# A rotary embedding on half of each head: three 8.4 MB slots with 64 KB rows on one DMA queue, instead of six 4.2 MB buffers with 32 KB rows

## The chip, the cores and the metric

The kernel runs on one core of one Trainium2 chip. The metric is the device time of one execution in microseconds (us). The profile's span is about 1.8 us shorter than that time (160.6 beside 162.34 us for the profiled run of the kernel before); spans are compared with spans only. All timed runs quoted are in the fast state with a granted clock of 1.0, except the two kernels named `gap_...`, which were run once and whose state is therefore unknown.

Executions of one kernel on one chip scatter by about 0.3 us, and now and then by more (one execution of the kernel before took 163.91 us). Each experiment was timed beside the kernel before, and that kernel's own median moved from 161.96 to 162.51 us between the sets of runs; times of different sets are compared by their ratio to the kernel before.

## The reference, cut to what matters

```python
# x: (16, 512, 16, 64) float32; cos, sin: (512, 32) float32
half_dim = 32
x1, x2 = x[..., :32], x[..., 32:]                # x2 is passed through
first  = x1[..., :16] * cos[..., :16] - x1[..., 16:] * sin[..., :16]
second = x1[..., :16] * sin[..., :16] + x1[..., 16:] * cos[..., :16]
return concatenate([first, second, x2], axis=-1)
```

x has 33.55 MB. Every byte comes in from HBM and goes out again, whether it is rotated or not: 67.1 MB for the DMA.

## The kernel before

A tile is 128 partitions by 32 KB (4.19 MB); there are eight tiles and six buffers. Six loads are queued at once. Each tile is rotated in place by four VectorE instructions, with PSUM as the scratch, and stored. Loads 6 and 7 wait for the store that frees their buffer. The constants come over GpSimd's queue.

```python
    K = 8
    NB = 6
    # ... views of x and out as (tile, partition, 8192 elements)
    nc.gpsimd.dma_start(out=stage[:, 0]..., in_=cosf)
    nc.gpsimd.dma_start(out=stage[:, 1]..., in_=sinf)
    # ... table = the constants spread to 128 partitions, four copies
    for t in range(NB):
        load(t)                                   # nc.sync.dma_start, 32 KB per partition
    for t in range(T):
        x1 = x_t[:, :, :, 0:HF]
        nc.vector.tensor_mul(out=b_t[:], in0=x1, in1=s)
        nc.vector.tensor_mul(out=x1, in0=x1, in1=c)
        nc.vector.tensor_sub(out=x1[..., 0:Q], in0=x1[..., 0:Q], in1=b_t[..., Q:HF])
        nc.vector.tensor_add(out=x1[..., Q:HF], in0=x1[..., Q:HF], in1=b_t[..., 0:Q])
        nc.sync.dma_start(out=of[t], in_=x_t...)
        if t >= 1 and t - 1 + NB < T:
            load(t - 1 + NB)
```

## Time and profile before

| | us |
|---|---|
| median of the first three runs | 162.21 (162.18 to 162.48) |
| span of the profiled run | 160.6 |
| VectorE busy | 107.9 (67%) |
| DMA queue q1, share of 16 engines' span | 97.8% |

From the page of the kernel before: busy time, the DMA row in 40 slices of 4 us (tenths of busy share, and GB/s), and the DMA queues (packets, MB, share).

```profile
span 160.6 us, 118 instructions
DVE 107.9 (67%) x36; POOL 1.4 (1%) x6
DVE  0025999999999999999999999982999000000000
DMA  7999999999999999999999999999999999999994
GB/s 245 424 408 392 424 490 392 392 514 400 392 465 449 392 392 482 433 392 449 465 392 433 433 441 408 449 441 416 441 441 408 441 449 416 441 441 424 416 449 180
DMA packets 2368, 67.24 MB, mean 419 GB/s; under 512 B 288, under 2 KB 288, under 8 KB 320
q1 hardware_dynamic: 2304, 67.11, 97.8%
```

The DMA row is full but for the first and last slice: the kernel is DMA-bound throughout. VectorE ends 36 us before the span does, so its idle time costs nothing. 2304 packets on q1 are 2048 of 32 KB and 256 that count semaphores.

The instruction groups of the kernel before, costliest first: line, engine, operation, shapes | busy us, mean ns | idle before and what ended it.

```profile
L73 DVE TENSOR_TENSOR b_t<-x_t,table 128x4096 f32<-128x4096 f32 x8 | 35.5, 4432 | 5.7 <-DMA x_t<-in_x_dram 5.5
L49 DVE COPY table<-stage 64x256 f32<-64x256 f32 x4 | 1.1, 287 | 10.6 <-DMA stage<-in_cos_dram 8.4
```

**The four sections that this text uses.** The trace keeps start, duration and size of every DMA packet. I cut each span at four points that can be read from them: the *head* (span start to the first packet of x), the *first phase* (the 25.2 MB of x, 6 x 4.19 MB, until the last of their packets has ended), the *rest* (the other 41.9 MB) and the *tail* (last packet's end to the end of the span). This is my arithmetic on the packet records, not a view of the profile. In the trace of before: head 1.75, first phase 60.36, rest 97.23, tail 1.23 us; together 160.57. In steady stretches a further 4.19 MB of loads takes 9.71 us and of stores 9.68 us.

### The profile page before, as it was taken

To read this page: it belongs to the slowest core of one execution; us is meant where nothing else is said; L and a number is where in the kernel's file an instruction comes from. 1 tells how busy PE (TensorE), PEld (TensorE's weight loads), DVE (VectorE), ACT (ScalarE), POOL (GpSimd) and SP (SyncE) were. 2 spreads that over 40 slices of the span, in tenths; PEclk is the share of its full clock that TensorE was granted. 3 is DMA by queue.
4 is the path that set the end of the run, shared out by engine and by line. 5 is a ranking of instruction groups with operands and counts; after the bars stand their busy time and mean duration, and the time that the engine had idled before them with its cause. 6 is when DMAs were issued, how large, how long until landed. Compare 5 with 4: busy or idle time off the path is not lost.

```text
span 160.6 us, 118 instructions
## 1 busy us (share of the span) xinstructions
DVE 107.9 (67%) x36; POOL 1.4 (1%) x6
## 2 busy tenths in 40 slices
DVE  0025999999999999999999999982999000000000
POOL 3000000000000000000000000000000000000000
DMA  7999999999999999999999999999999999999994
GB/s 245 424 408 392 424 490 392 392 514 400 392 465 449 392 392 482 433 392 449 465 392 433 433 441 408 449 441 416 441 441 408 441 449 416 441 441 424 416 449 180
DMA packets 2368, 67.24 MB, mean 419 GB/s; under 512 B 288, under 2 KB 288, under 8 KB 320
## 3 DMA queue, kind: packets, MB, share of 16 engines
q1 hardware_dynamic: 2304, 67.11, 97.8%
q0 software_dynamic: 64, 0.13, 0.2%
HBM read 33.69 MB, written 33.55 MB: 419 GB/s over the span
## 4 chain that ended last, share of the span: by engine, by line
DMA 52%; DVE 21%; issue 3%; DVEq 1%
DMA x_t<-in_x_dram 26%; DMA out_dram<-x_t 26%; DVE b_t L73 8%; DVE x_t L74 8%; DVE x_t L78 3%; DVE x_t L75 2%; DVEq L109 1%; DVEq L73 0%
## 5 line engine op out<-in xcount | busy, mean ns | idle before, releaser
L73 DVE TENSOR_TENSOR b_t<-x_t,table 128x4096 f32<-128x4096 f32 x8 | 35.5, 4432 | 5.7 <-DMA x_t<-in_x_dram 5.5
L74 DVE TENSOR_TENSOR x_t<-x_t,table 128x4096 f32<-128x4096 f32 x8 | 35.4, 4424 | 0.3
L75 DVE TENSOR_TENSOR x_t<-x_t,b_t 128x2048 f32<-128x2048 f32 x8 | 18.3, 2286 | 0.3
L78 DVE TENSOR_TENSOR x_t<-x_t,b_t 128x2048 f32<-128x2048 f32 x8 | 18.2, 2279 | 0.0
L49 DVE COPY table<-stage 64x256 f32<-64x256 f32 x4 | 1.1, 287 | 10.6 <-DMA stage<-in_cos_dram 8.4
L42 POOL DMA_DIRECT2D stage<-in_cos_dram x1 | 0.6, 648 | 0.8 <-PEq L109 0.8
L43 POOL DMA_DIRECT2D stage<-in_sin_dram x1 | 0.5, 518 | 0.0
L98 POOL MEMSET const-bfloat16-1.0<- 128x1 bf16 x1 | 0.1, 102 | 0.0
L98 POOL MEMSET const-float32-0.0<- 128x1 f32 x1 | 0.1, 98 | 0.2 <-issue 0.2
L98 POOL MEMSET const-float32-1.0<- 128x1 f32 x1 | 0.1, 99 | 0.0
L98 POOL MEMSET const-uint8-127<- 128x1 uint8 x1 | 0.1, 99 | 0.0
## 6 DMA issues: line engine op xcount, KB each, us to landing
x_t<-in_x_dram SPq DMA_DIRECT2D x8, 4096.0 KB, 30.2
out_dram<-x_t SPq DMA_DIRECT2D x8, 4096.0 KB, 41.9
stage<-in_cos_dram POOLq DMA_DIRECT2D x1, 64.0 KB, 7.2
stage<-in_sin_dram POOLq DMA_DIRECT2D x1, 64.0 KB, 9.3
```

Of the source, the lines that this page charges most:

```text
L42: nc.gpsimd.dma_start(out=stage[:, 0].rearrange("p k j -> p (k j)"), in_=cosf)
L43: nc.gpsimd.dma_start(out=stage[:, 1].rearrange("p k j -> p (k j)"), in_=sinf)
L49: nc.vector.tensor_copy(out=table[r * PB : (r + 1) * PB, t], in_=stage[:, t, :, 0:Q].unsqueeze(2).to_broadcast((PB, K, 2, Q)),)
L73: nc.vector.tensor_mul(out=b_t[:], in0=x1, in1=s)
L74: nc.vector.tensor_mul(out=x1, in0=x1, in1=c)
L75: nc.vector.tensor_sub(out=x1[:, :, :, 0:Q], in0=x1[:, :, :, 0:Q], in1=b_t[:, :, :, Q:HF])
L78: nc.vector.tensor_add(out=x1[:, :, :, Q:HF], in0=x1[:, :, :, Q:HF], in1=b_t[:, :, :, 0:Q])
L98: nc = _bacc.Bacc("TRN2", target_bir_lowering=False, num_devices=1)
L109: with _tile.TileContext(nc) as tc:
```

## The change

Its intent: the same bytes with half as many, twice as long rows, everything on one queue. Three slots of 8.39 MB; the constants come behind load 0 in the same queue; the first tile is stored in halves so that the last tile can be loaded into its place in halves; then three whole stores.

```diff
-    K = 8
+    K = 16
-    NB = 6
+    NS = 3
+    KC = K // 2
-    nc.gpsimd.dma_start(out=stage[:, 0]..., in_=cosf)
-    nc.gpsimd.dma_start(out=stage[:, 1]..., in_=sinf)
+    ring = const_pool.tile([P, NS, K, H, D], fp32)
+    load(0)
+    nc.sync.dma_start(out=stage[:, 0]..., in_=cosf)
+    nc.sync.dma_start(out=stage[:, 1]..., in_=sinf)
+    load(1)
+    load(2)
     # (the table's copies: four of 32x1024 instead of four of 64x256)
-    for t in range(NB):
-        load(t)
-    for t in range(T):
-        # ... rotate tile t
-        nc.sync.dma_start(out=of[t], in_=x_t...)
-        if t >= 1 and t - 1 + NB < T:
-            load(t - 1 + NB)
+    rotate(0, 0)
+    store(0, 0, KC)
+    rotate(0, KC)
+    store(0, KC, K)
+    load(3, 0, KC)
+    load(3, KC, K)
+    for t in range(1, T):
+        rotate(t, 0)
+        rotate(t, KC)
+        store(t)
```

(The moved body of the rotation is the same.)

More of the change, by code (lines that the diff above doesn't have):

```diff
@@ L29 @@
     REP = P // PB
-    NB = 6
+    R = H * D
+    NS = 3
+    KC = K // 2
     xf = x.rearrange("b s h d -> (b s h d)").rearrange("(t p f) -> t p f", t=T, p=P)
@@ L37, with rows @@
     const_pool = ctx.enter_context(tc.tile_pool(name="const", bufs=1))
-    x_pool = ctx.enter_context(tc.tile_pool(name="xp", bufs=NB))
     b_pool = ctx.enter_context(tc.tile_pool(name="bp", bufs=1, space=bass.MemoryType.PSUM))
+    ring = const_pool.tile([P, NS, K, H, D], fp32)
     stage = const_pool.tile([PB, 2, K, HF], fp32)
-    nc.gpsimd.dma_start(out=stage[:, 0].rearrange("p k j -> p (k j)"), in_=cosf)
-    nc.gpsimd.dma_start(out=stage[:, 1].rearrange("p k j -> p (k j)"), in_=sinf)
     table = const_pool.tile([P, 2, K, 2, Q], fp32)
-    for r in range(REP):
-        for t in range(2):
-            nc.vector.tensor_copy(
-                out=table[r * PB : (r + 1) * PB, t],
-                in_=stage[:, t, :, 0:Q].unsqueeze(2).to_broadcast((PB, K, 2, Q)),
-            )
+    def rows(t, lo, hi):
+        return ring[:, t % NS, lo:hi].rearrange("p k h d -> p (k h d)")
@@ new lines, in load, with store @@
+    def load(t, lo=0, hi=K):
+        nc.sync.dma_start(out=rows(t, lo, hi), in_=xf[t, :, lo * R : hi * R])
+    def store(t, lo=0, hi=K):
+        nc.sync.dma_start(out=of[t, :, lo * R : hi * R], in_=rows(t, lo, hi))
+    load(0)
+    nc.sync.dma_start(out=stage[:, 0].rearrange("p k j -> p (k j)"), in_=cosf)
+    nc.sync.dma_start(out=stage[:, 1].rearrange("p k j -> p (k j)"), in_=sinf)
+    load(1)
+    load(2)
+    for r in range(REP):
+        nc.vector.tensor_copy(
+            out=table[r * PB : (r + 1) * PB].rearrange("p t k c j -> p (t k) c j"),
+            in_=stage.rearrange("p t k j -> p (t k) j")[:, :, 0:Q]
+            .unsqueeze(2)
+            .to_broadcast((PB, 2 * K, 2, Q)),
+        )
@@ L53 @@
     C = table[:, 0].rearrange("p k c j -> p k (c j)")
     Sn = table[:, 1].rearrange("p k c j -> p k (c j)")
-    KC = 8
-    tiles = []
-    def load(t):
-        x_t = x_pool.tile([P, K, H, D], fp32, name="x_t")
-        nc.sync.dma_start(out=x_t.rearrange("p k h d -> p (k h d)"), in_=xf[t])
-        tiles.append(x_t)
-    for t in range(NB):
-        load(t)
-    for t in range(T):
-        x_t = tiles[t]
-        for k0 in range(0, K, KC):
-            x1 = x_t[:, k0 : k0 + KC, :, 0:HF]
-            c = C[:, k0 : k0 + KC].unsqueeze(2).to_broadcast((P, KC, H, HF))
-            s = Sn[:, k0 : k0 + KC].unsqueeze(2).to_broadcast((P, KC, H, HF))
-            b_t = b_pool.tile([P, KC, H, HF], fp32)
-            nc.vector.tensor_mul(out=b_t[:], in0=x1, in1=s)
-            nc.vector.tensor_mul(out=x1, in0=x1, in1=c)
-            nc.vector.tensor_sub(
-                out=x1[:, :, :, 0:Q], in0=x1[:, :, :, 0:Q], in1=b_t[:, :, :, Q:HF]
-            )
-            nc.vector.tensor_add(
-                out=x1[:, :, :, Q:HF], in0=x1[:, :, :, Q:HF], in1=b_t[:, :, :, 0:Q]
-            )
-        nc.sync.dma_start(out=of[t], in_=x_t.rearrange("p k h d -> p (k h d)"))
-        if t >= 1 and t - 1 + NB < T:
-            load(t - 1 + NB)
@@ new lines, in rotate @@
+    def rotate(t, k0):
+        x1 = ring[:, t % NS, k0 : k0 + KC, :, 0:HF]
+        c = C[:, k0 : k0 + KC].unsqueeze(2).to_broadcast((P, KC, H, HF))
+        s = Sn[:, k0 : k0 + KC].unsqueeze(2).to_broadcast((P, KC, H, HF))
+        b_t = b_pool.tile([P, KC, H, HF], fp32)
+        nc.vector.tensor_mul(out=b_t[:], in0=x1, in1=s)
+        nc.vector.tensor_mul(out=x1, in0=x1, in1=c)
+        nc.vector.tensor_sub(
+            out=x1[:, :, :, 0:Q], in0=x1[:, :, :, 0:Q], in1=b_t[:, :, :, Q:HF]
+        )
+        nc.vector.tensor_add(
+            out=x1[:, :, :, Q:HF], in0=x1[:, :, :, Q:HF], in1=b_t[:, :, :, 0:Q]
+        )
```

## The prediction

> **What bounds the kernel now.** The DMA engines. The DMA part of the profile's page shows queue q1 busy for 97.8% of 16 engines' span and 419 GB/s over 160.6 us; VectorE is busy 107.9 us (67%) and finishes at 124.7 us (timeline), 36 us before the end. In the trace's packet records a 32 KB packet takes 1213 ns (27.0 GB/s an engine); steady completions of successive 4.19 MB transfers are 9.68 us apart for stores and 9.71 us for loads, 433 and 432 GB/s. The Trainium skill, "DMA: Bandwidth & Descriptors", section "Where 436 GB/s comes from", gives 435.2 GB/s as the fabric's ceiling; this trace agrees to 0.7%. So 67.1 MB need 154.2 us at that ceiling and took 155.3 us plus about 2.3 us of extras: first transfer 1.7 us late (ramp, first packets 2.0 us instead of 1.2; constants in between) and about 0.8 us at the three places where a load is followed by a store. Head (1.75 us to the first packet) and tail (1.2 us after the last) are the rest.
>
> **What the change does.** The same bytes go through. It halves the number of big packets (2048 of 32 KB to mostly 64 KB), cuts x transfers from 16 to 10, moves the constants from the GpSimd queue behind the first 8.4 MB load, and enlarges the tiles from 4.19 to 8.39 MB in three slots. VectorE's rotations keep their shapes: 13.44 us per half, 107.6 us in all. The table copies grow: four of 32x1024 where four of 64x256 took 287 ns; estimate from that, at equal time per element, 1.1 us each, 4.5 us.
>
> **What lies on the critical path.** Only DMA continuity and packet efficiency. My schedule (estimates from these durations, us): load 0 and constants landed at 23.5; rotation from 28 to 136 without a pause; queue: load 1 and 2 to 62; store 0a and 0b 62 to 81; load 3a and 3b 81 to 101; store 1 to 120; store 2 to 140; store 3 to 159. Store 0a is ready at 41, 0b at 55; load 3a waits for 0a to land (about 72) while 0b still runs, load 3b waits for 0b while 3a runs; store 3 is ready at 136, 3 to 4 us before the engines reach it. So no bubble, and later VectorE work costs nothing.
>
> Gain: a packet costs 5 (stores) to 9 (loads) ns over its bytes at 435.2 GB/s; the skill's same page, section "Why small descriptors are slow", names a fixed cost of some cycles per packet. Up to 64 fewer packets an engine: 0.3 to 0.6 us, estimate 0.45. One load-to-store turn fewer and less interference of the constants: 0.2 us. Total -0.65 us of 162.2: 161.5 us, -0.4%.
>
> So 161.5 us, range 160.9 to 162.4; faster by over 2%: 0.02, within 2%: 0.94, slower by over 2%: 0.04.
>
> **What would show it right or wrong.** Right: about 1100 to 1400 packets; 64 KB packets near 2418 ns; DMA share 9 in every slice but the ends; VectorE idle about 27 us at the start, then busy to about 136 us; SP waits only, with DMA never idle. A DMA gap near 72 to 85 us would show load 3 waiting too long; one near 140 us, the last store coming too late.
>
> **What would make it wrong.** 64 KB runs cut into 32 KB packets (gain shrinks to 0.2 us); 64 KB packets or their larger row pitch running slower than 27 GB/s an engine; the constants landing late, or table copies far slower than estimated, so that the 3 to 4 us of slack before store 3 are gone; a longer ramp or slower turns.

## The result, and the profile after

| | before, us | after, us | ratio, 95% interval |
|---|---|---|---|
| first measurement, 6 runs each | 162.29 | 162.09 | 0.9987 [0.9969, 1.0004] |
| again, 11 and 6 runs | 162.22 | 161.92 | 0.9967 [0.9933, 1.0001] |

A ratio is the mean time of one kernel's fast runs over that of the other's in the same rounds, so it isn't quite the ratio of the medians. The gain is some 0.2 to 0.3 us, where 0.65 us was forecast; each interval just reaches 1.

The page of the changed kernel, the same lines as above:

```profile
span 160.2 us, 103 instructions
DVE 109.5 (68%) x36; POOL 0.2 (0%) x4
DVE  0000009999999999999999999999999995000000
DMA  8969989699699797999999999996996996996990
GB/s 262 524 262 524 524 295 524 262 524 507 278 524 475 311 524 327 458 393 434 483 393 401 483 425 393 524 524 262 524 507 278 524 507 278 524 491 295 524 491 33
DMA packets 1536, 67.24 MB, mean 420 GB/s; under 512 B 192, under 2 KB 192, under 8 KB 256
q1 hardware_dynamic: 1536, 67.24, 98.0%
```

The sixes and the swing from 262 to 524 GB/s are not gaps. A packet is counted in the slice in which it starts; sixteen engines start their 64 KB packets (2.42 us) almost together, so a 4 us slice holds sometimes one set, sometimes two. The packet records show all engines at work without a gap. Packets fell from 2368 to 1536, and the mean rate is 420 GB/s after 419. The work is the same, done at almost the same rate.

```profile
L79 DVE TENSOR_TENSOR b_t<-ring,table 128x4096 f32<-128x4096 f32 x8 | 35.5, 4432 | 0.3
L65 DVE COPY table<-stage 32x1024 f32<-32x1024 f32 x4 | 2.7, 683 | 23.9 <-DMA stage<-in_sin_dram 23.9
```

Those are the groups of the changed kernel. VectorE waits 23.9 us for the constants and then works without a pause until 134.2 us (timeline). The waits of the queue's own engine show that the stores were in the queue in time:

```profile
SPq L55 <- DVE ring L84: 80.8, 4, 26.5
SPq L52 <- DMA out_dram<-ring: 27.9, 2, 18.1
```

(Engine, line, what it waited for: us in total, times, longest.) SP waits long, but the DMA always has queued work meanwhile. The last store is issued at 134.2 us, and its packets start from 138.9 us on.

Here are the four sections for both kernels, two traces each, in us:

| | before | before, again | after | after, again | after - before, first pair / second pair |
|---|---|---|---|---|---|
| head | 1.75 | 1.74 | 1.74 | 1.75 | 0.00 / +0.01 |
| first phase (25.2 MB) | 60.36 | 60.43 | 60.12 | 60.15 | -0.24 / -0.28 |
| rest (41.9 MB) | 97.23 | 97.49 | 96.92 | 96.87 | -0.30 / -0.62 |
| tail | 1.23 | 1.23 | 1.41 | 1.40 | +0.18 / +0.18 |
| span | 160.57 | 160.89 | 160.19 | 160.17 | -0.37 / -0.72 |

(The profiled run of the second "before" was 162.66 us, above its kernel's median of 162.49, so the second pair overstates the gain.) Steady loads now take 9.675 us per 4.19 MB (9.71 before), and whole stores 9.66 us (9.68). That is the per-packet gain that was predicted: 6 x 0.039 + 6 x 0.022 = 0.37 us. But the 0.23 us that the loads contribute lie wholly in the first phase. That phase did become 0.24 to 0.28 us shorter, but the run with the old rows in the new order (runs_32k, below) is shorter by as much.

### The profile page after: what moved, and what is told of

It reads as the page before. It is cut to its first block, busy times and chain, and to the rows that moved or that the text cites. A ratio compares the mean times of both kernels' runs of the same rounds, so it can differ in the third digit from the quotient of the medians.

```text
span 160.2 us, 103 instructions
## 1 busy us (share of the span) xinstructions
DVE 109.5 (68%) x36; POOL 0.2 (0%) x4
## 2 busy tenths in 40 slices
DMA packets 1536, 67.24 MB, mean 420 GB/s; under 512 B 192, under 2 KB 192, under 8 KB 256
## 3 DMA queue, kind: packets, MB, share of 16 engines
q1 hardware_dynamic: 1536, 67.24, 98.0%
## 4 chain that ended last, share of the span: by engine, by line
DVE 61%; DMA 14%; issue 6%; DVEq 1%; SPq 0%
DVE b_t L79 22%; DVE ring L80 22%; DMA stage<-in_sin_dram 14%; DVE ring L84 10%; DVE ring L81 6%; DVE table L65 1%; DVEq L123 1%; SPq L58 0%; SPq L52 0%; DVEq L65 0%
## 5 line engine op out<-in xcount | busy, mean ns | idle before, releaser
L79 DVE TENSOR_TENSOR b_t<-ring,table 128x4096 f32<-128x4096 f32 x8 | 35.5, 4432 | 0.3
L80 DVE TENSOR_TENSOR ring<-ring,table 128x4096 f32<-128x4096 f32 x8 | 35.4, 4424 | 0.3
L65 DVE COPY table<-stage 32x1024 f32<-32x1024 f32 x4 | 2.7, 683 | 23.9 <-DMA stage<-in_sin_dram 23.9
L81 DVE TENSOR_TENSOR ring<-ring,b_t 128x2048 f32<-128x2048 f32 x8 | 18.3, 2286 | 0.3
L84 DVE TENSOR_TENSOR ring<-ring,b_t 128x2048 f32<-128x2048 f32 x8 | 18.2, 2279 | 0.0
```

The source lines that it names most:

```text
L65: nc.vector.tensor_copy(out=table[r * PB : (r + 1) * PB].rearrange("p t k c j -> p (t k) c j"), in_=stage.rearrange("p t k j -> p (t k) j" ...
L81: nc.vector.tensor_sub(out=x1[:, :, :, 0:Q], in0=x1[:, :, :, 0:Q], in1=b_t[:, :, :, Q:HF])
L84: nc.vector.tensor_add(out=x1[:, :, :, Q:HF], in0=x1[:, :, :, Q:HF], in1=b_t[:, :, :, 0:Q])
```

## The experiments

Two words for what follows: a *turn* is the place in the queue where a load is followed by a store, and a *stall* is what the last load packets of a run take beyond their steady time, averaged over the 16 engines.

### Repeats, and the constants moved

> The kernel before, unchanged, for the scatter. From its first trace: data 157.59 us from the first to the last 32 KB packet, head 1.75, tail 1.23 us; in the data, beyond a steady 9.71 us (load) and 9.68 us (store) per 4.19 MB: start 1.68 us, the three load-to-store turns 0.40, 0.28 and 0.11 us. If these terms are properties of the kernel they return within 0.1 us; if they are chance[...] they move by some tenths. Ratio 1.000 within 0.002.

> The changed kernel, unchanged, five rounds. Theory 1 (bookkeeping of the first trace): packets -0.37, turns -0.6, start with constants +0.41, tail +0.18, sum -0.37 us, ratio 0.9977. Rival: the first trace's turns were luck, sum near -0.1 us, ratio 0.9993. The trace is expected to show steady 9.675 us per 4.19 MB for loads and 9.66 for stores, and about 0.8 us of extra where the constants pass.

Measured: before again 162.49 us (ratio 1.0003 to itself), after again 161.92 us. The medians of identical kernels differ by up to 0.27 us (162.49 against 162.22), which is the scatter to keep in mind. In the traces the terms of before did move. Its start term (time to 4.19 MB beyond the steady 9.71) was 1.68 and then 2.14 us, and its first turn took 0.40 and then 0.01 us extra. Their sum, 2.08 and 2.15 us, hardly moved. That was the first hint. The two forecasts for the repeat of the changed kernel, ratios of 0.9977 and 0.9993, both lie in the measured interval (0.9933 to 1.0001), so the times don't decide between them. Its trace repeats: every section returned within 0.06 us, and the steady rates as well.

```diff
# const_gpsimd: the changed kernel with
-    nc.sync.dma_start(out=stage[:, 0]..., in_=cosf)      # between load(0) and load(1)
+    nc.gpsimd.dma_start(out=stage[:, 0]..., in_=cosf)    # sin likewise
```

> The changed kernel with the constants back on the GpSimd queue, wanted early. Theory 1: a burst of 2 KB packets between two loads in one queue costs 0.34 us of its own and then about 0.5 us of slow first packets of load 1; on the other queue they overlap the start: start term 2.08 falls to about 1.65, time -0.4 us against the changed kernel. Rival: constants cost the same wherever they pass (0.3 to 0.8 us): the start term stays within 0.15 us of 2.08 and the time is equal.

Measured: 162.33 us (ratio 0.9996), nothing gained over before. What the start cost stayed at 2.05 us (1.63 + 0.42), as the rival said; theory 1 fell. The rest grew to 97.25 us.

```diff
# const_first: the changed kernel with
-    load(0)
     nc.sync.dma_start(out=stage[:, 0]..., in_=cosf)
     nc.sync.dma_start(out=stage[:, 1]..., in_=sinf)
+    load(0)
```

> The changed kernel with the constants first in the same queue, before load 0. Theory 1: the slow first packets come once after every burst of small packets or idle stretch, so here they are paid once only: start term about 1.3 us (0.34 for the constants, 0.9 for the slow first packets), time -0.7 us against the changed kernel less what the two extra issues put before load 0 (0.9 us of issue, partly hidden). Rival: the issue time of the two constants delays load 0 by its full 0.9 us, so nothing or +0.2 us.

> The kernel with the constants first, once more, for a second trace. If the 1.32 us at the turn after load 2 belongs to this order it returns (above 0.9 us); if it was chance it falls among the 0.0 to 0.4 us of the other kernels and the time is about 1 us shorter than 163.5.

Measured: 163.52 us (ratio 1.0077) and 163.13 us (1.0061): slower, with both intervals above 1, though by less than 2%. The head grew from 1.74 to 2.69 us, because load 0 is issued behind the two small transfers. The start term did fall by 0.9 to 1.0 us, to 1.08 and 1.23 us. But then load 2 ended 1.32 and 1.09 us later than its steady rate gives, because its last packets were slow. The saving before the turn was taken back at the turn.

### Run length and tail, each alone

```diff
# runs_32k: every load and store of the changed kernel in two halves (32 KB rows)
     def load(t, lo=0, hi=K):
+        if hi - lo > KC:
+            load(t, lo, lo + KC)
+            load(t, lo + KC, hi)
+            return
```

> The changed kernel with every 64 KB transfer cut into its two 32 KB halves, order, queue, table and slots as in the changed kernel: the run length alone undone. Theory 1 (run length is worth its per-packet cost): steady 9.71 us per 4.19 MB for loads and 9.68 for stores again, data +0.37 us over the changed kernel's 157.03, and the tail back from 1.41 to 1.23 us, so about +0.2 us in time, 162.2. Theory 2 (fewer slow turns come with the 64 KB runs): the turns grow from 0.15 back to 0.6 to 0.8 us as well, about +0.7 us. Rival (turns follow from the order of transfers): turns stay near 0.15 us.

Measured: 162.03 us, ratio 0.9979 [0.9961, 0.9998] to before. So the changed order with the old row length does as well as the changed kernel. Steady rates went back to 9.71 and 9.68 us, the rest to 97.07 (+0.2), the tail to 1.19 (-0.2). The first phase stayed at 60.155 us although it had 0.23 us more of packet cost in it. So the 64 KB rows do what was predicted per packet, but set against this run they gain only 0.14 to 0.20 us, all of it in the rest, and the tail takes back 0.21. In the time they bring nothing measurable.

```diff
# tail_halves: the changed kernel, the last store in halves
-        store(t)
+        store(t) if t < T - 1 else (store(t, 0, KC), store(t, KC, K))
```

> The changed kernel with only the last store cut into two 32 KB-run halves. Theory: the longer tail (1.41 against 1.23 us from the last packet's end to the end of the span) comes with the 64 KB packets at the end; it returns to 1.23, data +0.02, time -0.15 us, 161.8. Rival: the tail comes from the 8.4 MB size or from chance and stays at 1.4.

Measured: 162.17 us (ratio 0.999), tail 1.37 us; the theory fell. The instruction records of the tails point to the cause. After the last transfer SP steps through a list of waits for all DMA semaphores, one step each 55 to 68 ns. In the changed kernel, and in this one, the last store's semaphore stands early in the list, so that four more steps follow it (the last began 0.26 us after the landing); in before it was in the last pair (0.08 us). That is 0.18 us less or more of list, and 0.35 to 0.42 us from last packet to landing in all of them. No run moved the semaphore alone.

### Does what is saved before the turn count?

```diff
# no_const: the changed kernel without the constants (wrong result on purpose)
-    nc.sync.dma_start(out=stage[:, 0]..., in_=cosf)
-    nc.sync.dma_start(out=stage[:, 1]..., in_=sinf)
+    nc.vector.memset(stage[:], 1.0)
```

> The changed kernel without loading the constants (the table is filled with ones, the result is wrong on purpose). Theory A (terms add): the 0.85 us that the constants cost between load 0 and load 1 vanish, turns stay near 0.15: data 156.2 us, time 161.1. Theory B (what is saved before the first load-to-store turn is given back at it, as in the run with the constants first, where the turn took 1.32 us): the turn grows by 0.5 us or more and the time stays above 161.6.

Measured: 161.92 us, ratio 0.9978 [0.9957, 1.0000]. Theory B: the 0.85 us that the constants had taken vanished from between load 0 and load 1, load 1 landed at 41.96 instead of 42.96 us, and then load 2's last packets stalled by 1.22 us (1.14 us by the end of the transfer). Load 2 landed at 62.43 us, and 62.31 us in the changed kernel.

Ordinary table, from the packet records: when 16.8 MB (4 x 4.19) and 25.2 MB had ended, counted from the first packet of x, in us.

```
kernel               16.8 MB   25.2 MB    mean of load 2's last 16 packets, us
before                40.53     60.36     (32 KB packets)
before_again          41.00     60.43     (32 KB packets)
after                 40.77     60.12     2.44
after_again           40.81     60.15     2.53
const_gpsimd          40.75     60.25     2.54
const_first           39.78     60.45     3.68
const_first_again     39.88     60.31     3.53
runs_32k              40.51     60.16     (32 KB packets)
tail_halves           40.70     60.49     2.76
no_const              39.87     60.36     3.64
burst_mid2            39.89     60.21     2.68
burst_turn            39.80     60.49     3.63
copy_only             39.94     60.33     3.48
gap_turn              39.81     59.14     2.42
```

After 16.8 MB the kernels differ by 1.2 us. After 25.2 MB all but the last row lie within 0.4 us. A steady 64 KB packet takes 2.42 us; where a kernel was early, its last packets took up to 3.7 us. Sums of terms don't describe this phase: what was saved early was lost again at its end. But this holds only as finely as one trace can show it. tail_halves has the same queue as the changed kernel up to this point, and yet it took 60.49 us where the changed kernel took 60.12 and 60.15.

### What kind of limit is it?

```diff
# turn_early: no_const with the first turn moved ahead of load 2
     load(0)
     load(1)
-    load(2)
     rotate(0, 0); store(0, 0, KC); rotate(0, KC); store(0, KC, K)
+    load(2)
     load(3, 0, KC); load(3, KC, K)
```

> No constants loaded (wrong on purpose), and the first stores moved ahead of load 2: load 0, load 1, store 0a, 0b, load 2, 3a, 3b, then the stores. Without constants the first three loads and then a store showed a 1.14 us stall in the last packets of load 2, 58 to 62 us into the span. Floor (a load phase can't average more than about 25.2 MB in 60.3 us, 418 GB/s, and settles at its end): stall about 0.3 us at 41 us, about the same after load 3. Unbroken run (the first switch from loads to stores costs 1.1 us however long the run, unless a burst of small packets broke it): 1.1 us at 41 us. Fixed event (something slows the DMA 58 to 62 us into the program): nothing at 41 us, 1.1 us at 58 to 62 in whichever transfer is then in flight.

Measured: the stall was 1.03 us and came at 41 us into the span, and a second of 0.64 us (packets; 0.77 in the transfer's end) after loads 2 and 3. Nothing happened between 58 and 62 us. That refutes a fixed event and a floor in proportion to the bytes (0.3 us expected at 41 us). The time was 162.87 us (ratio 1.0045).

```diff
# burst_mid2 / burst_turn: no_const with the two small loads, into a spare tile
     load(0); load(1)
+    small()          # burst_mid2
     load(2)
+    small()          # burst_turn
```

> No constants used (wrong on purpose), but the same two small transfers as a dummy burst between load 1 and load 2 instead of between load 0 and load 1. Floor: the burst costs 0.85 us where it is and the phase still ends 60.1 to 60.5 us after the first packet, so the stall at the turn falls to 0 to 0.4 us. Additive: burst 0.85 and turn 1.14, phase end near 61.2 us.

> As before, with the dummy burst between load 2 and store 0a, at the turn itself (wrong on purpose). Floor or drain: the burst lies inside the stall and is nearly free, stores begin 59.7 to 60.4 us after the first packet, time as without constants, 161.9. Additive: stores begin near 61.0 us and the time is 162.6.

Measured: with the burst between loads 1 and 2, 60.21 us for the first phase and 162.04 us in all; it costs 0.76 us where it is, and the turn only 0.24 us. With the burst at the turn, load 2's last packets stalled 1.21 us *before* the small loads began, and the burst then came on top (rest 97.21 against 96.76 us in no_const; 162.47 us). So a burst in the middle of the run replaces most of the stall, and a burst at its end doesn't; "nearly free at the turn" was wrong.

```diff
# copy_only: no_const without rotate(...): loads and stores only
-    rotate(0, 0)     # and all others
```

> No constants and no rotation at all: loads and stores only, in the same order (wrong on purpose). If VectorE's traffic in the on-chip memory makes the stall at the turn, it goes (below 0.3 us) and the time falls to about 160.9. If it belongs to the transfers alone, it stays near 1.1 us and the time near 161.9; the head, steady rates and tail stay as they are too.

Measured: stall 1.07 us, first phase 60.33, 162.02 us. VectorE's traffic isn't the cause. It also shows that VectorE is free here: without any rotation, the kernel takes the same time as no_const.

### The transfer that waits behind the run

```diff
# gap_turn: copy_only, but all stores read slot 2, so the first waits until load 2 has landed
-    store(0, 0, KC); store(0, KC, K); load(3, 0, KC); load(3, KC, K)
+    store(0); store(1); store(2)      # each from slot 2
+    load(3); store(3)                 # through slot 2
```

> Copies only (wrong on purpose): three loads of 8.4 MB in one unbroken run, and nothing behind them in the queue, because the first store waits until load 2 has landed. Interference (the transfer queued behind the run disturbs the last load packets): no stall, the 25.2 MB end 59.2 us after the first packet. End of run (the last packets of a long load run are slow whatever follows): stall of 1.0 to 1.3 us again, end at 60.2 to 60.5 us.

> Copies only, through one slot, each transfer waiting for the one before: four load runs of 8.4 MB and four store runs, each started and ended by an idle queue. Steady rates say 19.33 us for a load and 19.31 us for a store from first to last packet plus 1.2 us of slow first packets and stagger for loads. If the end of a load run costs 1.0 us at every length, a load run takes 21.5 us; if it needs a long run, 20.5 us or less. Store runs tell whether stores have such a start at all: about 19.4 us if not.

Measured in gap_turn: no stall. Sixteen last packets took 2.418 to 2.421 us, and 25.2 MB ended after 59.14 us. Here is, for the changed kernel, for no_const and for gap_turn, the answer of the profile for the line of the loads: the last number is the time from issue to landing of the slowest, which is load 2.

```profile
DMA to landing us min/median/max: 19.1/22.4/59.8
```

```profile
DMA to landing us min/median/max: 19.1/21.9/60.8
```

```profile
DMA to landing us min/median/max: 21.8/31.3/59.6
```

Load 2 was issued at 2.56, 1.63 and 1.64 us. So it landed at 62.3, 62.4 and 61.2 us: the two kernels with a store waiting behind load 2 land together, although the first of them carried the constants as well; the one with nothing behind is 1.2 us earlier. The views of two windows, no_const and then gap_turn (columns: duration, busy us of VectorE and GpSimd, clock, DMA share, GB/s by packet start) show the same:

```profile
58.00:59.00 1.00, 0.97 (x2) 0.00 (x0) 1.00 3.16 918
59.00:60.00 1.00, 1.00 (x1) 0.00 (x0) 1.00 0.00 0
60.00:61.00 1.00, 1.00 (x2) 0.00 (x0) 1.00 0.00 0
61.00:62.00 1.00, 1.00 (x1) 0.00 (x0) 1.00 0.92 393
```

```profile
58.00:59.00 1.00, 0.00 (x0) 0.00 (x0) 1.00 2.27 983
59.00:60.00 1.00, 0.00 (x0) 0.00 (x0) 1.00 0.00 0
60.00:61.00 1.00, 0.00 (x0) 0.00 (x0) 1.00 0.01 0
61.00:62.00 1.00, 0.00 (x0) 0.00 (x0) 1.00 0.00 0
62.00:63.00 1.00, 0.00 (x0) 0.00 (x0) 1.00 2.49 1049
```

Each line covers one microsecond. Its DMA share counts all the time of the packets that start in it, as a share of 16 engines, and can so be above 1. From 58 to 59 us, 14 packets of 64 KB start in no_const (918 GB/s) and 15 in gap_turn (983 GB/s). The shares, 3.16 and 2.27, make 3.6 us a packet in the first and 2.42 us in the second: the same kind of packets, longer. The gap that gap_turn pays instead (its first store packet comes 1.22 us after the last load packet) is as long as the stall was, so waiting is no cure.

Measured in gap_short: load runs of 8.4 MB between two idle stretches took 20.45 to 20.54 us, that is 1.1 to 1.2 us beyond the steady 19.33, with slow first packets (0.54 to 0.80 us per engine) and no slow last ones. Store runs took 19.55 us, 0.24 us beyond their steady 19.31, and their first packets were slow by 0.04 us only. So loads have a start of 1.1 us to pay and stores have little.

```diff
# jit_2rows: no_const; load 2 in two parts, and the first store held back by GpSimd
-    load(2)
+    load(2, 0, 14)
+    load(2, 14, K)
     rotate(0, 0)
+    nc.gpsimd.tensor_sub(out=mark, in0=last_of_part_1, in1=last_of_part_1)   # 0
+    nc.gpsimd.tensor_add(out=held, in0=held, in1=mark)                       # held: one column of tile 0
     store(0, 0, KC)
```

> No constants (wrong on purpose), rotation kept; load 2 cut into rows 0 to 13 and rows 14, 15 of each partition, and the first store held back by two tiny GpSimd operations until the first part of load 2 has landed, so that it is queued about 1.5 us after that and 0.9 us before the last 2.4 us of loads end. If a transfer queued behind the run for a long time stalls its last packets, the first 25.2 MB end near 59.2 to 59.6 us after the first packet instead of 60.36, stores follow within 0.3 us and the time falls from 161.92 by 0.6 to 1.0 us, to about 161.1. If any transfer queued in time stalls them, nothing is won: end at 60.2 or later, 161.9 or more.

> The same with one row (1.2 us of loads) behind the mark: the store's packets should come 0.3 to 0.5 us after the last load packet. If interference is the cause, load packets show no stall (end 59.15), and a gap of 0.3 to 0.5 us follows; time about 161.3. If the end of a long run were slow whatever is queued, end at 60.2 and later.

Measured in jit_2rows: the store was issued at 59.42 us, 0.55 us after the first part of load 2 had landed. The first phase ended after 59.29 us, 1.06 us sooner than in no_const, and the stores followed at once; the stall was gone, as the interference theory says. But the time was 163.75 us (ratio 1.0099), 1.8 us worse than no_const's. In its trace the next two turns, store 0 to load 3 and load 3 to store 1, had 0.89 and 1.28 us of slow packets, where no_const had 0.00 and 0.02. The stall had moved and grown. The expected time of 161.1 us was a miss.

jit_1row didn't test what it was meant to: the build put the second half of tile 0's store, which doesn't wait for the mark, ahead of the first (issues at 49.56 and 60.85 us). So a store was waiting all the same; load 2's last packets were slow again, the phase ended after 60.33 us, and the time was 162.31 us.

> The correct kernel: the changed one with the first store held back in the same way (two rows). The constants burst stays between load 0 and load 1, where it costs 0.85 us, and the turn behind it took only 0.0 to 0.44 us in three traces, so at most 0.3 us is to be won: 161.7 to 162.1.

Measured: 165.99 us (ratio 1.024), far slower. Here the hold took too long. From the timeline of jit_real:

```profile
58.16 4.42 DVE L82 TENSOR_TENSOR ring<-ring,table 128x4096 f32<-128x4096 f32 x1
60.07 2.58 POOL L94 TENSOR_TENSOR mark<-ring 128x1 f32<-128x1 f32 x1 [59.62 <-DMA ring<-in_x_dram]
62.72 0.19 POOL L95 TENSOR_TENSOR ring<-ring,mark 128x1 f32<-128x1 f32 x1
62.94 0.82 SPq L55 DMA_DIRECT2D out_dram<-ring  x2
```

A GpSimd operation on one element per partition lasted 2.58 us, until just after VectorE's multiplication ended at 62.58 us; the next like it took 0.19 us. The Trainium skill, "SBUF — State Buffer", section "Who interferes with whom", says that a VectorE instruction with two SBUF inputs contends with a GpSimd instruction that reads SBUF, and this line agrees: the multiplication reads ring and table. In jit_2rows the same GpSimd operation took 0.20 us, beside a subtraction (L82 of that kernel) whose second input lies in PSUM. The store came 2.9 us after its mark, the DMA engines stood idle for about 2 us, and later turns were slow as well (0.9 and 0.8 us). No version here beats the changed kernel; those with the changed order and 161.9 to 162.2 us can't be told apart. The kernel before itself had a median of 161.96 us in this last set.

### What is shown, and what isn't

Shown: the stall is in the last packets of a long run of loads (16.8 or 25.2 MB, without a break) when a store is already waiting behind it in the queue, directly or, in burst_turn, behind two small loads. Loads alone waiting there are not enough: the last packets of load 1 took 2.42 us in burst_mid2, ahead of small loads. And it isn't there in every kernel: in the changed one, whose run the constants interrupt, these packets took 2.44 and 2.53 us with a store waiting. It isn't VectorE (copy_only), not a fixed time after the start (turn_early), and not the end of the run itself (gap_turn). Held-back stores remove it at that turn (jit_2rows). A burst of small loads within the run takes its place in part.

Open: what happens inside the DMA engines. The Trainium skill, "DMA: Bandwidth & Descriptors", section "Two DMAs through the same engine are not ordered", describes transfers of one queue as pipelined, with separate read and write sides. A read side that runs on into the waiting transfer while load data are still on their way would fit, but no run here looks inside. Nor do I know why a burst of small loads 20 to 40 us earlier nearly removes the stall, or why a smooth first turn made the later turns slow. Each of these statements rests on one trace of a kernel or two.

## Why the prediction was right or wrong

Right:

- *"The DMA engines"* bound the kernel before and after; share 97.8% and 98.0%. The no-change class was right, and the time lay within the range, 162.09 and 161.92 us against 160.9 to 162.4. That range holds the kernel before as well (162.2), so it would have been met with no gain at all.
- *"A packet costs 5 (stores) to 9 (loads) ns over its bytes"*: the steady rates gave 0.37 us in all for 0.45 predicted; 64 KB packets took 2418 ns, as written. Both kernels' rates, 432 to 434 GB/s, agree within 0.7% with the 435 GB/s that the Trainium skill, "DMA: Bandwidth & Descriptors", section "Where 436 GB/s comes from", names.
- *"So no bubble"*: VectorE ran from 26.7 to 134.2 us for 28 to 136 predicted, load 3's halves came without an idle gap, and the last store was queued 4.6 us before its turn.

Wrong, and with it the size of the change: *"Total -0.65 us"* (161.5 us). Measured were -0.20 and -0.30 us by the medians, -0.37 and -0.72 us by the spans of the traces (the second pair overstates it). The failing step is the sum of *"Gain"*. Its terms were added as if every nanosecond saved anywhere on a busy DMA came off the end, and the tail was taken to stay at 1.2 us. Term by term:

- *"estimate 0.45"* for the packets is the term that failed most. The steady rates show 0.37 us. runs_32k undoes the row length alone, and against it only 0.14 to 0.20 us appears, in the rest. The first phase holds 0.23 us of the packet gain, and it ended at the same time: 60.16 us with 32 KB rows (runs_32k), 60.12 and 60.15 us with 64 KB rows. It is 0.24 and 0.28 us shorter than in the kernel before, but it is so with the old rows too. That this phase takes back a saving is shown for the 0.85 us of the constants (no_const). For the 0.23 us it is argued only, since single traces of it differ by up to 0.37 us (tail_halves).
- *The tail*, which the prediction left out of the sum, took back 0.18 us against the kernel before and 0.21 us against runs_32k, most likely by the order of the waits at the end. So the longer rows came to nothing: the span is 160.15 us in runs_32k, 160.19 and 160.17 us in the changed kernel.
- *"One load-to-store turn fewer and less interference of the constants: 0.2 us"* was about right as a sum: the new order with the old rows (runs_32k) was 0.29 us below the kernel before by the medians. Half of its reason was wrong. The constants cost the same or more in their new place: start and constants 2.09 and 2.10 us, against 1.68 and 2.14 us. Their cost isn't separable either: without them (no_const) the first phase took 60.36 us, not less. The rest gained 0.17 and 0.49 us beyond its 0.13 us of packets.

One rival stays open. A plain sum with the packets at 0.37 and the tail put in is -0.37 - 0.2 + 0.18 = -0.39 us, which fits the first pair of traces (-0.37) without any saving being taken back. The runs are too few to say how much of the shortfall is due to which; the tail is certain, as it repeats to 0.01 us.

Off the path, *"1.1 us each, 4.5 us"* for the table's copies was wrong: 683 ns each and 2.8 us. Equal time per element ignores the fixed part. A straight line through the two sizes (287 ns for 256 elements, 683 for 1024) gives an estimate of 0.52 ns per element and 155 ns fixed.

## What to carry to other kernels

When the DMA engines are busy from end to end, longer rows save only their per-packet cost, here 5 to 10 ns on 1.2 us, and that is worth a trial only when nothing larger is left. Don't add up savings inside a run of loads: look at when the run's last packets end, and at what is queued behind them, because a stall there can swallow a saving before it (here 0.85 us in no_const). And compare the tails: a change in the order of transfers can move 0.2 us there. Before you explain a few tenths of a microsecond, run the same kernel twice and see which terms of your bookkeeping return.

## What the Trainium skill lacked or had wrong

- "DMA: Bandwidth & Descriptors": no section tells that an unbroken load run's last packets can stall when a store waits behind it in the same queue (3.4 to 3.7 us instead of 2.42 us per 64 KB packet, 1.0 to 1.3 us in all; none with an empty queue behind, and 0.02 to 0.34 us where small loads came within the run).
- The same page, "Why small descriptors are slow": halving the packets from 8 to 4 an engine per 4.19 MB saved 0.022 us for stores and 0.039 us for loads, which makes a fixed cost of about 5 and 10 ns a packet; the page doesn't tell the two apart.
- The same page: a load that starts on an idle queue has first packets 0.54 to 0.80 us slower than steady ones, a store 0.04 us (gap_short). No section gives this difference.
- No page gives the cost of a kernel's own list of waits for its DMA semaphores at its end: 55 to 68 ns for each step, so that the place of the last store's semaphore seems to be worth up to 0.2 us (tails of 1.23 and 1.41 us).
